# A hybrid encoder layer: the sums of w2's quarters, the second MLP product's order and the end of the kernel rearranged

## The chip, the cores and the metric

The kernel runs on one core of one Trainium2 chip. A core has a matrix engine (TensorE, PE, with its weight loads as PEld), a vector engine (VectorE, DVE), a scalar engine (ScalarE, ACT), a general engine (GpSimd, POOL) and a sync engine (SyncE, SP) that here issues transfers. The metric is the device time of one execution in microseconds (us), taken as the median of several runs.

## The reference, cut to what matters

One layer of a streaming encoder is applied to 1024 prompt tokens and to 8 x 16 sample tokens that carry states of earlier chunks; here all 1152 tokens go through together. All is float32.

```python
proj = x @ w_in                      # (1152, 1024) after a LayerNorm; its columns feed four mixers
mix  = concat(ssd(proj), mlstm(proj), rglru(proj), gla(proj))      # (1152, 2048); SSD and RG-LRU: causal conv4 first
x    = layer_norm(ALPHA * x + mix @ w_out, ln1_g, ln1_b)
hid  = square(relu(x @ w1 + b1))                                  # (1152, 4096)
x    = layer_norm(ALPHA * x + hid @ w2 + b2, ln2_g, ln2_b)        # written out, with 8 states per token kind
```

mLSTM, GLA and SSD are computed chunk by chunk (9 chunks of 128 tokens, the ninth is the sample), with a state carried from one prompt chunk to the next.

## The kernel before, in words

**How a product is made.** A float32 product is three products of reduced-precision parts: `mm3` issues hi·hi, hi·lo and lo·hi into one PSUM bank. The high part of an operand is a copy by ACT, the low part a subtraction by DVE (`wl<-wr,wh`, `mlo<-mr,mh`, `wo<-wq,wo`, `ol<-ar,oh`). So each weight passes SP (load), ACT (high part) and DVE (low part) before PE can use it.

**Stages**, with their place in the time of before:

- `dense_first` (to about 60 us): input LayerNorm, transposes, the first five column blocks of w_in in chunks of 384 tokens, three chunks (c = 0, 1, 2) each. Each block's `evac` empties its PSUM bank. For the first two blocks of the SSD convolution (`conv_block`), `evac` at c = 0 also transposes the carried conv states on PE (`pcs<-ident,cst`, line 737); they come by DMA into `cst`.
- SSD (to about 230), mLSTM (230 to 560), GLA (560 to 640), RG-LRU (640 to 860). PE works on the columns of w_in for a later mixer (`block`) while the small steps of the present mixer are put among them: `tick()` is called at fixed places of each block and hands out steps. In mLSTM a chunk i goes through `stA`, `stB` and `stC`; `stB` makes `y` (ACT, DVE, POOL), and `stC`, called three chunks behind `stA`, transposes `y` on PE (`py`). In GLA a chunk ends with the update of the state `St` on DVE and its scaled copies `glB`, which the next chunk's product reads.
- `w_out` and LN1 (865 to 1075): operands `mh`, `mlo` (of the mixed result `mr`) and `wh`, `wl`; `acc` gathers the products, and at the end each row tile of 128 tokens gets its LayerNorm (`st`, `rs`, ACT `acc<-acc,rs`), is stored to `xn_d` by SP and transposed on PE (`pt<-ident,acc`) for the MLP.
- The first MLP product, x @ w1 (1075 to 1440), by the seven-product scheme of Strassen and Winograd on quarters of each matrix, in 16 column blocks j. `mlp_a` and `mlp_b` issue a block's matmuls; `q_load` and `q_prep` load and prepare w1's quarters (`wq`, `wo`) two blocks ahead; `more()` is called among the matmuls and hands out a step of preparation. Results go through `hid` (DVE, ACT) to DRAM (`hid_d`) and sums of their quarters (`sq`) to `s_d`.
- The second MLP product, hid @ w2 (1440 to 1803), by the same scheme with products 1 to 7 of 8 units each (a unit is 256 of the inner dimension); the sums T1 to T4 of w2's quarters are read from DRAM (`t_d`). The sample tokens have a plain product, handed out with units of products 1, 0 (a name for units of the sample alone), 2 and 3.
- The end: LN2 of the last rows and their stores.

**The sums of w2's quarters** (`w2_sums`, lines 1631 to 1670): for each of 32 groups four loads of 128x256 by SP into buffers `w2q`, four subtractions on DVE, four stores to `t_d`, all 128 loads and 128 stores issued by SP. The steps are in the list `behind`, of which each `tick()` takes one; they lie from the start of mLSTM to the start of RG-LRU (225 to 668 us).

**What sets the order.** A scheduler of the tile framework orders each engine's instructions by a model of its own; only where `pinned` names an engine does that engine keep the order of the program. It names DVE, ACT and PE in `dense_first` (until line 360) and in one place of the MLP, and all four engines from line 2372 on, for the end. Between these, the order in which the code makes the instructions is only a wish. An engine works through its list in order: a waiting instruction holds up all behind it.

Of the kernel before, what the change touches and what calls it, by code (L numbers as in the profile page):

```python
# [39 lines left out]
STT = (7, 6)  # L40
NG5 = 0
PIN = 'VATG'
LOG = ((4, 0), (4, 1))
CHUNKS = (tuple(range(6)), (6, 7))
NQ = 3
HT = NTOK // 2
# [4 lines left out]
def tile_trunk(ctx: ExitStack, tc: tile.TileContext, I, O, dbg=None):  # L51
# [169 lines left out]
    behind = []  # L221
# [495 lines left out]
    def conv_block(store, key, st_in, nrow, ch0, wcol, bcol, act, o_p, o_s, early=False):  # L717
# [11 lines left out]
        def evac(c, ps):  # L729
            if c == 0:  # L730
                raw = S("raw", (P, SW))
                d["raw"] = raw
                V.memset(raw[:, 0:3], 0.0)
                sv = raw[:, 1027:1179].rearrange("p (b s) -> p b s", s=19)
                d["sv"] = sv
                cs = d["cs"] if early else load()
                pt = pm("pcs")
                T.transpose(pt[:, 0:24], cs[0:24, :], ident[0:24, 0:24])
                A.activation(sv[:, :, 0:3], pt[:, 0:24].rearrange("p (b j) -> p b j", j=3), AF.Copy)
            raw = d["raw"]  # L740
# [36 lines left out]
        def state():  # L777
            raw, sv = d["raw"], d["sv"]
            cs = Dt("cso", 27)
            A.activation(cs[:, 0:3], raw[:, PT:PT + 3], AF.Copy)  # L780
            A.activation(cs[:, 3:27].rearrange("p (b j) -> p b j", j=3), sv[:, :, LS:LS + 3], AF.Copy)
            pt = pm("pco")
# [298 lines left out]
    def ml_steps(h):  # L1081
# [22 lines left out]
        def stB(i):  # L1104
# [41 lines left out]
            y = Dt("y", P)  # L1146
            A.activation(y, ti[:, 0:P], AF.Square, scale=r[:, 0:1], accum_out=r[:, 1:2])
# [3 lines left out]
            G.tensor_scalar(y, ti[:, 0:P], r[:, 3:4], None, op0=OP.mult)  # L1151
            d["y", i] = y
# [36 lines left out]
        for s in range(NT + 3):  # L1189
            def f(s=s):  # L1190
# [6 lines left out]
                if 3 <= s <= NT + 2:  # L1197
                    stC(s - 3)
# [97 lines left out]
    def gl_steps(p):  # L1296
# [21 lines left out]
        def stB(i):  # L1318
# [3 lines left out]
            if i < 8:  # L1322
# [11 lines left out]
                if i:  # L1334
                    G.tensor_scalar(St, St, sc[:, 1, i:i + 1], None, op0=OP.mult)
                    V.scalar_tensor_tensor(St, pS, sc[:, 2, i:i + 1], St, op0=OP.mult, op1=OP.add)
                else:
                    V.tensor_scalar(St, pS, sc[:, 2, 0:1], None, op0=OP.mult)
                if i < 7:
                    for h in range(2):  # L1340
                        hs = slice(64 * h, 64 * h + 64)
                        V.tensor_scalar(glB[hs, h, :], St[hs], sc[hs, 0, i + 1:i + 2], None, op0=OP.mult)
# [129 lines left out]
    def rg_steps(j):  # L1472
# [15 lines left out]
        def gates(c):  # L1488
            def f():
# [7 lines left out]
                if c < 2:  # L1497
                    split(c + 1)
# [45 lines left out]
        return [g0] + [w] * 5 + [gates(0)] + [w] * 0 + [gates(1)] + [w] * 0 + [gates(2), e1, e2, e3]  # L1544
# [86 lines left out]
    def w2_sums():  # L1631

        out = []
        src = (("11", 0, 0), ("12", 0, 512), ("22", KF // 2, 512), ("21", KF // 2, 0))
        for k in range(KF // 2):
            for c in (0, 256):
                q = {}

                def load(k=k, c=c, q=q):
                    for nm, k0, c0 in src:  # L1640
                        q[nm] = C("w2q")[:, 0:256]
                        D.dma_start(q[nm], w2[(k0 + k) * P:(k0 + k + 1) * P, c0 + c:c0 + c + 256])

                def sub(dst, a, b, q=q):
                    V.tensor_tensor(q[dst], q[a], q[b], op=OP.subtract)

                def store(n, nm, k=k, c=c, q=q):
                    D.dma_start(t_d[n][k, :, c:c + 256], q[nm])

                def f2(sub=sub):  # L1650
                    sub("11", "12", "11")
                    sub("12", "22", "12")

                def f3(sub=sub, store=store):
                    store(0, "11")
                    store(2, "12")
                    sub("22", "22", "11")
                    sub("21", "22", "21")

                def f4(store=store):  # L1660
                    store(1, "22")
                    store(3, "21")

                if out:
                    last = out.pop()
                    out.append(lambda load=load, last=last: (last(), load()))
                else:
                    out.append(load)
                out += [lambda: None, f2, f3, f4]
        return out  # L1670

    behind.extend(w2_sums())
# [21 lines left out]
    while behind:  # L1694
        behind.pop(0)()
# [106 lines left out]
    def x_rest(k):  # L1802
# [11 lines left out]
        x_split("S4", k, a12)  # L1814

# [243 lines left out]

    for j in range(KF // 2):  # L2060
        def more():
            if prep[j] and j == 0:
# [8 lines left out]
        while j + 1 in prep and prep[j + 1]:  # L2071
            more()

# [56 lines left out]
    def lo_engine(p, u):  # L2130
        return G if (p, u - tail[0]) in LOG else V

    def w_prep(i):
        if i < len(units):
            p, u = units[i]
            opw[p, u] = parts(wr.pop((p, u)), lo_engine(p, u))

    def a_prep(i):
        if i < len(units):
            p, u = units[i]  # L2140
            if prods[p][0]:
                opa[p, u] = parts(ar.pop((p, u)), lo_engine(p, u))
# [18 lines left out]
    def sample(p, u):  # L2161
        if p in samp:
            h, g = samp[p]
            (ah, al), (wh, wl) = hs[u // 2], opw[p, u]
            for k in range(2):
                n = (u % 2) * 2 + k
                mm3(sps[h], (ah[:, g, n], al[:, g, n]), (wh[:, k], wl[:, k]),
                    u == k == g == 0, u == NU - 1 and k == 1 and g == 0)

    acc = {}  # L2170

    def part_of(p, t):

        nm, ix = {1: ("a1", None), 5: ("a5", None), 6: ("a6", None), 2: ("top", 0), 3: ("top", 1), 4: ("bot", 0),
                  7: ("bot", 1)}[p]
        key = (nm, t // 2 if ix is None else t)
        if key not in acc:
            acc[key] = S3(nm)
        return acc[key][:, t % 2 if ix is None else ix, :]

    def evac(p, t, ps, first):
        a = part_of(p, t)
        if first and p in (1, 5, 6):
            if t % 2:
                V.tensor_copy(a, ps)
            else:
                A.activation(a, ps, AF.Copy)
        else:
            V.tensor_tensor(a, a, ps, op=OP.subtract if p == 4 else OP.add)
# [10 lines left out]
    def res_make(i):  # L2200
# [3 lines left out]
        if 4 <= i < 8:  # L2204
            G.tensor_tensor(r[:, left], r[:, left], r[:, right], op=OP.subtract)
# [20 lines left out]
    def ln_b(i):  # L2226
        rs = lnrs[i]
        G.tensor_scalar(rs[:, 2:3], lnst[i][0][:, 24:25], rs[:, 1:2], -1.0, op0=OP.mult, op1=OP.mult)
        A.activation(row(i), row(i), AF.Identity, scale=rs[:, 1:2], bias=rs[:, 2:3])

    def ln_g(i):
        G.tensor_tensor(row(i), row(i), g2, op=OP.mult)

    def ln_stt(i, n):

        mean, rs = lnst[i][0][:, 24:25], lnrs[i]
        for cs in (left, right):
            a = row(i)[:, cs]
            if n == 0:
                V.scalar_tensor_tensor(a, a, mean, g2[:, cs], op0=OP.subtract, op1=OP.mult)  # L2240
# [212 lines left out]
```

## Time and profile before

| what | value |
|---|---|
| median of 3 runs | 1825.93 us (1824.7 to 1827.39) |
| profiled execution | 1824.16 us, span 1822.4 us |
| granted clock of PE, mean | 0.986 |
| PE busy | 1739.7 us (95%) |
| DVE busy | 1220.2 us (67%) |
| ACT busy | 748.3 us (41%) |
| POOL busy | 598.9 us (33%) |
| transfers | 252.5 MB, mean 139 GB/s |

Span is the time from the first to the last recorded event of the profiled execution; the device time of that same execution is 1.8 us longer. Busy shares are averages over stages that differ much: PE has no gap at all in some stages and stands often in others. Waits are inferred from semaphore events, with the releaser that came last.

### The profile page before, as it was taken

The numbers are of one execution on the slowest core, as the hardware profiler recorded it, in microseconds if no ns is written. First come the engines' busy times: TensorE is split into PE (matmuls) and PEld (weight loads), VectorE is DVE, ScalarE is ACT, GpSimd is POOL, SyncE is SP. The second block draws the span as 40 slices with busy tenths as digits, with TensorE's granted clock in tenths as the row PEclk, the third lists the DMA queues.
The fourth block names the chain that finished last, engine by engine and source line by source line (L and its number), as shares of the span: only waits on it lengthen the run. The fifth ranks groups of instructions, "written<-read, shape, count | busy, mean of one in ns | idle before, by whom it ended". The sixth has DMA issues, their size and how long they took to land. (4 is left out here: it accounts for less than half of the span.)

```text
span 1822.4 us, 28131 instructions
## 1 busy us (share of the span) xinstructions
PE 1739.7 (95%) x10439; PEld 1580.7 (87%) x10439; DVE 1220.2 (67%) x2263; ACT 748.3 (41%) x1463; POOL 598.9 (33%) x558
## 2 busy tenths in 40 slices
PE   6999999999999999998999998999999999999995
PEld 5898989999989889897887888999999988888884
DVE  6867776644573654678777579666666678856569
ACT  4544433332341322365542275444444443433331
POOL 1123223522531313234255026433333135430047
PEclk8999999999999999999999999999999999999998
DMA  5132343546434350211445222554443696664542
GB/s 167 49 108 62 106 126 91 182 150 182 150 109 142 108 146 12 78 39 61 160 131 187 76 93 82 186 180 167 145 145 128 220 324 212 214 235 164 186 150 93
DMA packets 226961, 252.53 MB, mean 139 GB/s; under 512 B 27834, under 2 KB 171340, under 8 KB 226824
## 3 DMA queue, kind: packets, MB, share of 16 engines
q1 hardware_dynamic: 213000, 215.08, 37.4%
q10 hardware_dynamic: 13824, 35.66, 5.1%
q8 instruction: 82, 1.34, 0.3%
q14 instruction: 55, 0.45, 0.1%
HBM read 172.59 MB, written 76.33 MB: 137 GB/s over the span
## 5 line engine op out<-in xcount | busy, mean ns | idle before, releaser
L66 PE MATMUL pd<-xh,wh 128*128 128x384 f32 x936 | 330.1, 353 | 2.6 <-ACT xh L66 2.3
L66 PE MATMUL pd<-xh,wl 128*128 128x384 f32 x936 | 318.7, 340 | 0.0
L66 PE MATMUL pd<-xl,wh 128*128 128x384 f32 x936 | 311.0, 339 | 0.3 <-DVE xl L66 0.3
L66 PE MATMUL pm<-xo,wo 128*128 128x288 f32 x1680 | 232.2, 297 | 9.3 <-DVE wo L66 6.1
L66 PEld LDWEIGHTS pm<-xo,wo 128*128 128x128 f32 x1680 | 227.1, 190 | 10.7 <-DVE wo L66 7.3
L66 PEld LDWEIGHTS pd<-xh,wh 128*128 128x128 f32 x936 | 177.8, 190 | 8.4 <-ACT xh L66 3.3
L66 PEld LDWEIGHTS pd<-xl,wh 128*128 128x128 f32 x936 | 177.2, 190 | 1.9 <-issue 1.0
L66 PEld LDWEIGHTS pd<-xh,wl 128*128 128x128 f32 x936 | 177.2, 189 | 0.1
L66 POOL TENSOR_TENSOR wq<-wq 128x512 f32<-128x512 f32 x64 | 94.5, 1477 | 168.6 <-DVE wo L66 152.6
L66 PE MATMUL pd<-xo,wo 128*128 128x288 f32 x1008 | 140.3, 296 | 0.1
L66 PEld LDWEIGHTS pd<-xo,wo 128*128 128x128 f32 x1008 | 136.8, 189 | 0.3 <-ACT hid L66 0.3
L66 DVE TENSOR_TENSOR wo<-wq,wo 128x512 fp32r<-128x512 f32 x112 | 102.0, 930 | 31.3 <-ACT wo L66 30.6
L66 DVE TENSOR_TENSOR ol<-w2r,oh 128x1024 fp32r<-128x1024 f32 x62 | 97.9, 1586 | 26.5 <-ACT oh L66 10.0
L66 DVE TENSOR_TENSOR wl<-wr,wh 128x1024 fp32r<-128x1024 f32 x63 | 87.6, 1392 | 26.3 <-ACT wh L66 17.9
L66 ACT ACTIVATE oh<-ar 128x1024 fp32r<-128x1024 f32 x56 | 59.2, 1057 | 105.1 <-DVE ol L66 29.1
L66 DVE TENSOR_TENSOR ol<-ar,oh 128x1024 fp32r<-128x1024 f32 x54 | 78.1, 1446 | 33.1 <-ACT oh L66 28.8
L66 ACT ACTIVATE oh<-w2r 128x1024 fp32r<-128x1024 f32 x64 | 67.2, 1052 | 58.6 <-DVE ol L66 31.4
L66 PE MATMUL pd<-oh,ol 128*128 128x512 f32 (+1 forms) x228 | 89.5, 392 | 0.0
L66 PE MATMUL pd<-ol,oh 128*128 128x512 f32 (+1 forms) x228 | 89.3, 392 | 0.0
L66 PE MATMUL pd<-oh 128*128 128x512 f32 (+1 forms) x228 | 89.0, 391 | 0.0
L66 PE MATMUL pm<-oh,ol 128*128 128x512 f32 (+1 forms) x224 | 87.8, 392 | 0.0
L66 PE MATMUL pm<-ol,oh 128*128 128x512 f32 (+1 forms) x224 | 87.6, 391 | 0.0
(420 smaller groups left out, 4019.6 us busy)
## 6 DMA issues: line engine op xcount, KB each, us to landing
wr<-in_w_in_dram SPq DMA_DIRECT2D x46, 512.0 KB
wq<-in_mlp_w_dram SPq DMA_DIRECT2D x72, 256.0 KB
hid_d<-hid ACTq DMA_DIRECT2D x32, 576.0 KB
w2q<-in_mlp_w_dram SPq DMA_DIRECT2D x128, 128.0 KB
t_d<-w2q SPq DMA_DIRECT2D x128, 128.0 KB
s_d<-sq ACTq DMA_DIRECT2D x64, 256.0 KB
w2r<-in_mlp_w_dram SPq DMA_DIRECT2D x32, 512.0 KB
w2r<-t_d SPq DMA_DIRECT2D x32, 512.0 KB
```

The lines of the kernel that those rows point to most:

```text
L66: r = f(*a, **k)
```

## The change

1. **The sums of w2's quarters** are made in the first MLP product: `w2_sums` gets three steps a group (load, subtract, store), four buffers of its own (`NWQ = 4`) in the MLP's pool, and its stores are issued by ACT. `more()` takes one step from j = 2 on; what is left comes after the last block. The `behind` list in `tick` is gone. T4 has the other sign, and product 4 is added where it was subtracted.
2. **The second MLP product**: before, all products ran over units 0 to 5, then over units 6 and 7, with their results emptied and gathered twice. Now products 1, 2, 6, 5, 3 run over all 8 units, one after the other (sample-only units `0` among those of 6), 4 and 7 over units 0 to 4. LN2 of rows 0 to 3 and of the sample is in a list `later`, of which each unit of the following products takes up to two steps.
3. **The end**: for each of the last four row tiles, product 7 and then product 4 over units 5 to 7, and then that row's LN2; the last row's product 4 in two halves of 256 columns.
4. **Smaller moves**: the conv states' transposes (`pcs`) at c = 2, not c = 0; the copies `cso` of the conv's new states a step before their transpose; mLSTM's `y` in place in `ti`, and `stC` four chunks behind `stA`, not three; in GLA the state's update at high priority; in RG-LRU the split of a chunk's operand for the gates a step earlier.

The diff, cut to its core:

```diff
-        if behind:
-            behind.pop(0)()
...
+            if c == 2:
                 pt = pm("pcs")
-                T.transpose(pt[:, 0:24], cs[0:24, :], ident[0:24, 0:24])
...
+                T.transpose(pt[:, 0:24], d["cs"][0:24, :], ident[0:24, 0:24])
...
-            st += [taps(c, 0, 2), taps(c, 2, 4)]
+            st += [taps(c, 0, 2), taps(c, 2, 4) if c < 2 else lambda c=c: (taps(c, 2, 4)(), kept())]
...
-            G.tensor_scalar(y, ti[:, 0:P], r[:, 3:4], None, op0=OP.mult)
-            d["y", i] = y
+            G.tensor_scalar(ti[:, 0:P], ti[:, 0:P], r[:, 3:4], None, op0=OP.mult)
+            d["y", i] = ti[:, 0:P]
...
-                if 3 <= s <= NT + 2:
-                    stC(s - 3)
+                if 4 <= s <= NT + 3:
+                    stC(s - 4)
...
+                with tc.high_priority():
+                    if i:
+                        V.scalar_tensor_tensor(St, pS, sc[:, 2, i:i + 1], St, op0=OP.mult, op1=OP.add)
...
-        return [g0] + [w] * 5 + [gates(0)] + [w] * 0 + [gates(1)] + [w] * 0 + [gates(2), e1, e2, e3]
+        return [g0] + [w] * 4 + [lambda: split(1), gates(0)] + [w] * 0 + [gates(1)] + [w] * 0 + [gates(2), e1, e2, e3]
...
+                def load(k=k, c=c, q=q):
+                    for nm, k0, c0 in src:
+                        q[nm] = s2.tile([P, 256], F32, tag="W", name="w2q", bufs=NWQ)
+                        D.dma_start(q[nm], w2[(k0 + k) * P:(k0 + k + 1) * P, c0 + c:c0 + c + 256])
+                def sub(dst, a, b, q=q):
+                    V.tensor_tensor(q[dst], q[a], q[b], op=OP.subtract)
+                def store(n, nm, k=k, c=c, q=q):
+                    A.dma_start(t_d[n][k, :, c:c + 256], q[nm])
+                def subs(sub=sub):
+                    sub("11", "12", "11")
+                    sub("12", "22", "12")
+                    sub("22", "22", "11")
+                    sub("21", "21", "22")
+                out += [load, subs, stores]
...
+    sums = w2_sums()
     for j in range(KF // 2):
         def more():
+            if j > 1 and sums:
+                sums.pop(0)()
...
-    order, order_end = (1, 5, 6, 4, 0, 7, 2, 3), (2, 3, 0, 1, 6, 5, 7, 4)
-    tail = CHUNKS[-1]
-    units = [(p, u) for us in CHUNKS for p in (order_end if us is tail else order) for u in us]
+    tail = (5, 6, 7)
+    units = ([(p, u) for p in (1, 2) for u in range(NU)] + [(p, u) for u in range(NU) for p in (6, 0)]
+             + [(p, u) for p in (5, 3) for u in range(NU)] + [(p, u) for p in (4, 7) for u in range(tail[0])]
+             + [(p, u) for p in (7, 4) for u in tail])
...
+    def second(t, parts_):
+        i = 4 + t
+        for cs in parts_:
+            ps = bank()
+            tile_prod(ps, 4, t, cs.start, cs.stop)
+            add(acc["bot", t][:, 0, cs], ps[:, cs])
             ln_stats2(i, cs)
         ln_a(i)
...
+    for t in range(4):
+        first(t)
+        if t:
+            ln_c(3 + t, left)
+            ln_c(3 + t, right)
+        second(t, lh if t == 3 else (left,))
+        if t < 3:
+            ln_b(4 + t)
+    ln_b(7, left)
+    ln_stt(7, right, 0)
+    ln_stt(7, right, 1)
+    ln_c(7, left)
```

How it moves instructions, at three places.

PE's order at the end of the first chunk of `dense_first`, before (`xh`, `xl` are the parts of the normed input, `wh`, `wl` those of w_in, `pd` a product's bank):

```order
L66 MATMUL pd<-xh_103,wh 128x384
L66 MATMUL pd<-xh_103,wl 128x384
L66 MATMUL pd<-xl_111,wh 128x384
L66 MATMUL pcs<-ident,cst 128x24
L66 MATMUL pd<-xl_111,wh 128x384
L66 MATMUL pcs<-ident,cst 128x24
L66 MATMUL pd<-xh_96,wh 128x384
L66 MATMUL pd<-xh_96,wl 128x384
```

And now, at the end of the third chunk:

```order
L63 MATMUL pd<-xh_103,wh 128x384
L63 MATMUL pd<-xh_103,wl 128x384
L63 MATMUL pd<-xl_111,wh 128x384
L63 MATMUL pcs<-ident,cst 128x24
L63 MATMUL pd<-xl_111,wh 128x384
L63 MATMUL pcs<-ident,cst 128x24
L63 MATMUL pd<-xl_111,wh 128x384
```

The two transposes have moved from the end of the first chunk to the end of the third, some 180 matmuls further on.

DVE's order in the last quarter of the `w_out` stage, before (`acc` gathers products, `mlo` is the low part of the mixed result):

```order
L66 TENSOR_TENSOR acc<-acc,pd 128x512
L66 TENSOR_TENSOR mlo<-mr,mh 128x1024
L66 TENSOR_TENSOR acc<-acc,pd 128x512 x2
L66 TENSOR_TENSOR mlo<-mr,mh 128x1024
L66 TENSOR_TENSOR acc<-acc,pm 128x512
L66 TENSOR_TENSOR acc<-acc,res 128x1024
L66 TENSOR_TENSOR acc<-acc,pm 128x512
L66 TENSOR_TENSOR mlo<-mr,mh 128x1024
```

And now, at the same place:

```order
L63 TENSOR_TENSOR mlo<-mr,mh 128x1024
L63 TENSOR_TENSOR w2q<-w2q 128x256 x3
L63 TENSOR_TENSOR acc<-acc,pd 128x512
L63 TENSOR_TENSOR w2q<-w2q 128x256
L63 TENSOR_TENSOR acc<-acc,pd 128x512
L63 TENSOR_TENSOR mlo<-mr,mh 128x1024
L63 TENSOR_TENSOR w2q<-w2q 128x256 x2
L63 TENSOR_TENSOR acc<-acc,pm 128x512
L63 TENSOR_TENSOR acc<-acc,res 128x1024
L63 TENSOR_TENSOR w2q<-w2q 128x256 x2
L63 TENSOR_TENSOR acc<-acc,pm 128x512
L63 TENSOR_TENSOR w2q<-w2q 128x256
```

The scheduler draws the first 10 or 11 of the 32 groups forward, out of the MLP's loop into the end of `w_out`, two loops ahead of where the code makes them; SP's loads of `w2q` stand there between those of `mr`, and ACT's stores to `t_d` between `mh` and `acc`. Some 9 more subtractions stand among the splits `xo` at the start of the MLP, the others among the first product's blocks.

DVE's order at the very end, before (`res` holds the rows, `st` and `rs` their statistics, `pd` and `pm` banks):

```order
L66 BN_STATS st<-res 128x6
L66 TENSOR_TENSOR res<-res,pm 128x256
L66 BN_STATS st<-res 128x6
L66 BN_AGGR st<-st 128x2
L66 TENSOR_SCALAR rs<-st 128x1
L66 SCALAR_TENSOR_TENSOR res<-res,st,g_17257 128x512 x2
L66 TENSOR_TENSOR res<-res,bb_17259 128x1024 x2
L66 SCALAR_TENSOR_TENSOR res<-res,rs,bb_17259 128x512 x2
L66 SCALAR_TENSOR_TENSOR res<-res,st,g_17257 128x512 x2
L66 SCALAR_TENSOR_TENSOR res<-res,rs,bb_17259 128x512 x2
```

And now:

```order
L63 BN_STATS st<-res 128x6
L63 TENSOR_TENSOR res<-res,pd 128x256
L63 BN_STATS st<-res 128x6
L63 BN_AGGR st<-st 128x2
L63 TENSOR_SCALAR rs<-st 128x1
L63 SCALAR_TENSOR_TENSOR res<-res,st,g_16539 128x512
L63 SCALAR_TENSOR_TENSOR res<-res,rs,bb_16541 128x512
L63 TENSOR_TENSOR res<-res,g_16539 128x512
L63 TENSOR_TENSOR res<-res,bb_16541 128x512
```

Behind the last addition of a product stood the last steps of four rows; now there are those of one row only.

## Rows read from the trace of the kernel before

**Rows 1.** the page, busy time of each engine

```profile
PE 1739.7 (95%) x10439; PEld 1580.7 (87%) x10439; DVE 1220.2 (67%) x2263; ACT 748.3 (41%) x1463; POOL 598.9 (33%) x558
```

**Rows 2.** PE in order: start, length, operation, [idle before <-releaser]

```profile
32.03 0.27 PE L66 MATMUL pcs<-ident,cst 24*128 24x24 f32 x1 [5.80 <-DMA cst<-in_state_ssd_conv_dram]
```

**Rows 3.** busy time by stretch: engines (count), PEclk, DMA share, GB/s

```profile
32.00:39.00 7.00, 6.97 (x24) 6.53 (x25) 0.00 (x0) 1.22 (x5) 0.00 (x0) 0.54 0.76 190
```

**Rows 4.** waits of PE, 60 to 230 us: total, times, longest

```profile
PE pco L66 <- ACT cso L66: 1.5, 1, 1.5
```

**Rows 5.** waits of PE, 230 to 640 us

```profile
PE py L66 <- POOL y L66: 7.3, 9, 2.4
PE pb L66 <- DVE E L66: 3.6, 6, 1.3
PE pb L66 <- DVE glB L66: 2.0, 3, 1.4
```

**Rows 6.** the tile w2q: ns min/median/max, first and last start; idle before it

```profile
L66 DVE TENSOR_TENSOR w2q<-w2q x128: 401/424/692, 230.9 to 665.7; 128x256 f32<-128x256 f32 x128
L1648 SPq DMA_DIRECT2D t_d<-w2q x128: 319/346/4178, 231.6 to 668.0; - x128
...
  DMA w2q<-in_mlp_w_dram: 32.4, 22
```

**Rows 7.** waits of PE, 800 to 1125 us

```profile
PE pgt L66 <- DVE gxl L66: 2.6, 3, 1.2
...
PE pt L66 <- ACT acc L66: 0.6, 1, 0.6
```

**Rows 8.** waits of DVE, 1001 to 1061 us

```profile
DVE mlo L66 <- ACT mh L66: 9.4, 3, 4.0
DVE acc L66 <- PE pd L66: 6.6, 5, 3.2
DVE acc L66 <- PE pm L66: 4.6, 3, 2.3
```

**Rows 9.** busy time by stretch, second half

```profile
1000.00:1075.00 75.00, 74.41 (x355) 61.25 (x354) 48.03 (x89) 29.80 (x41) 9.19 (x10) 1.00 0.22 81
1075.00:1125.00 50.00, 40.61 (x275) 39.09 (x274) 45.89 (x44) 32.15 (x57) 32.96 (x19) 0.90 0.18 53
1125.00:1440.00 315.00, 315.00 (x2377) 315.00 (x2376) 204.16 (x337) 152.94 (x269) 110.96 (x74) 1.00 0.48 164
1440.00:1803.00 363.00, 362.34 (x1594) 295.08 (x1592) 259.37 (x237) 138.23 (x142) 121.06 (x59) 1.00 0.58 198
```

**Rows 10.** the tile wq, whole run

```profile
L66 DVE TENSOR_TENSOR wo<-wq,wo x112: 635/688/1922, 1065.5 to 1416.6; 128x512 fp32r<-128x512 f32 x112
```

**Rows 11.** waits of DVE, 1130 to 1440 us

```profile
DVE sq L66 <- ACT hid L66: 36.3, 27, 2.3
DVE wo L66 <- ACT wo L66: 29.1, 27, 1.7
DVE hid L66 <- PE pm L66: 19.3, 25, 4.2
```

**Rows 12.** all engines in time order, the end

```profile
1802.27 0.28 PE L66 MATMUL pm<-ol,oh 128*128 128x256 f32 x1
...
1802.39 0.28 PE L66 MATMUL pm<-oh,ol 128*128 128x256 f32 x1
...
1808.14 0.40 DVE L66 TENSOR_TENSOR res<-res,pm 128x256 f32<-128x256 f32 x1
...
1809.46 3.56 DVE L66 SCALAR_TENSOR_TENSOR res<-res,st,g 128x512 f32<-128x512 f32 x2
...
1811.76 1.00 POOL L66 TENSOR_TENSOR rs<-rs,nhalf 128x1 f32<-128x1 f32 x1
...
1815.97 3.65 SPq L2243 DMA_DIRECT2D out_dram<-res  x4
...
1817.86 1.40 DVE L66 SCALAR_TENSOR_TENSOR res<-res,rs,bb 128x512 f32<-128x512 f32 x2
```

More of the change, by code (lines that the diff above doesn't have):

```diff
@@ L39 @@
 NS3 = 9
[L40 to L41 removed]
 PIN = 'VATG'
[L43 to L44 removed]
 NQ = 3
+NWQ = 4
 HT = NTOK // 2
@@ L1188, in ml_steps @@
         out = []
-        for s in range(NT + 3):
+        for s in range(NT + 4):
             def f(s=s):
@@ L1629, in pair @@
         nb[0] += 2
[L1631 to L1672, printed above, removed]
     ml_n0()
@@ L1814, in x_rest, with w2_sums, stores @@
         x_split("S4", k, a12)
+    def w2_sums():
+        out = []
+        src = (("11", 0, 0), ("12", 0, 512), ("22", KF // 2, 512), ("21", KF // 2, 0))
+        for k in range(KF // 2):
+            for c in (0, 256):
+                q = {}
+                def load(k=k, c=c, q=q):
[11 more added lines that the diff above has]
+                    sub("21", "21", "22")
+                def stores(store=store):
+                    for n, nm in enumerate(("11", "22", "12", "21")):
+                        store(n, nm)
+                out += [load, subs, stores]
+        return out
     wq, wo = {}, {}
@@ L2072, in tile_trunk @@
             more()
+    while sums:
+        sums.pop(0)()
     s2x.close()
@@ L2167, in sample @@
                 mm3(sps[h], (ah[:, g, n], al[:, g, n]), (wh[:, k], wl[:, k]),
-                    u == k == g == 0, u == NU - 1 and k == 1 and g == 0)
+                    u == k == g == 0, u == NU - 1 and k == g == 1)
     acc = {}
[L2172 to L2189, printed above, removed]
     def row(i):
@@ L2224, in ln_a @@
         rsqrt_to(rs[:, 1:2], rs[:, 0:1])
[L2226 to L2240, printed above, removed]
-            else:
-                V.scalar_tensor_tensor(a, a, rs[:, 1:2], bb2[:, cs], op0=OP.mult, op1=OP.add)
-                D.dma_start(out_of(i, cs), a)
@@ L2315, in tile_trunk @@
             V.tensor_tensor(ba, ba, b2, op=OP.add)
[L2316 to L2320 removed]
+        if i % 3 == 1:
+            if i > 1 and made:
+                res_make(made.pop(0))
+            if todo:
+                res_load(todo.pop(0))
+        if p == 5 and u == 0:
             g2 = vec_bc("g2", I["ln2_g"][0])
@@ L2323, in tile_trunk @@
         sample(p, u)
-        if end and p == 5:
-            break
+        for _ in range(2):
+            if later:
+                later.pop(0)()
         if not p:
             continue
-        if cu == 0:
+        if u == 0:
             banks = [bank() for _ in range(4)]
         (ah, al), (wh, wl) = opa[p, u], opw[p, u]
+        n = NU if p in (1, 2, 6, 5, 3) else NU - len(tail)
         for k in range(2):
@@ L2333, in tile_trunk, with tile_prod @@
                 ts = slice(t * P, (t + 1) * P)
[L2334 to L2336 removed]
+                mm3(banks[t], (ah[:, k, ts], al[:, k, ts]), (wh[:, k], wl[:, k]), u == k == 0, u == n - 1 and k == 1)
+        if u < n - 1:
             continue
[L2338 to L2362 removed]
+        for t in range(4):
+            evac(p, t, banks[t])
+        if p == 3:
+            for h, cs in enumerate((left, right)):
+                later.append(lambda h=h, cs=cs: (add(acc["smp"][:, h], sps[h]), ln_stats2(8, cs)))
+            later.append(lambda: ln_a(8))
+            later.append(lambda: ln_b(8))
+            later.append(lambda: ln_c(8))
+    while later:
+        later.pop(0)()
+    prep_to(len(units))
+    def tile_prod(ps, p, t, c0=0, c1=512):
         ts = slice(t * P, (t + 1) * P)
```

211 lines of the change are left out of this document (83 added, 128 removed).

## Prediction

> **What bounds the kernel now.** I read the page first. PE is busy for 1739.7 of 1822.4 us [rows 1], so in this trace at most 82.7 us can be won without taking matmuls away, and the change takes none away. What counts is therefore where PE stands, and for whom. Then I read PE's waits by stage, and busy time by stretch.
>
> Four places make up most of it. In the first stage PE stands 5.80 us for the DMA of `cst` [rows 2], and after it runs at a granted clock of 0.54 for 7 us [rows 3]. In mLSTM and GLA it waits in many small pieces, 7.3 us for `y`, 3.6 for `E`, 2.0 for `glB` [rows 5]. At the start of the MLP it is busy for 40.61 of 50 us, while DVE is busy for 45.89 [rows 9]. The end is bare: the last matmul begins at 1802.39 [rows 12], the span ends at 1822.4. In both MLP products PE has nearly no gap, 315.00 of 315 and 362.34 of 363 us [rows 9]; there nothing can be won and something lost. So the change takes work from stages with gaps and puts it into stages without any, and the question is whether the vector engine can hide it there.
>
> **The change part by part.** The sum is made against the profiled execution, 1824.16 us.
>
> *Conv states at c = 2.* The transposes stood in front of the second chunk's matmuls, and the data came at 32.03. They now come some 180 matmuls later, by when it has long landed. The 5.80 us go; what is late next (a weight's low part, by PE's order) these rows don't price, and I allow it 1 us. The stretch at 0.54 lost 7 x 0.46 = 3.2 us against full clock [rows 3], and a pause of 1 us instead of 5.8 before it may spare up to that. Ends: -4 to -9; I take -7.
>
> *`cso` earlier:* one wait of 1.5 us [rows 4]; 0 to -1.5, I take -1.
>
> *mLSTM and GLA.* DVE loses 128 subtractions of 0.424 us = 54 us here, and 32.4 us of standing for `w2q` in 22 waits [rows 6]; as DVE works in order, each of these held up the small chains behind it. `stC` one chunk later gives `y` a whole chunk more, the high priority brings `glB` forward. Against PE stand 7.3 + 3.6 + 2.0 = 12.9 us [rows 5]. Ends: 0 (the chains are late by themselves) and -13; the waits are short and many, as a shared in-order engine makes them, so I take -10. The 128 loads and 128 stores also leave SP here, which can only help the loads of w_in behind them.
>
> *RG-LRU's split a step earlier:* 2.6 us in three waits for `gxl` [rows 7]; 0 to -2.6, I take -2.
>
> *The end.* Before, behind the last matmul came the last addition at 1808.14, 5.7 us late because DVE had a backlog, and then 11 us of steps for four rows, to 1819.26; the span ends 3.1 us after that [rows 12]. Now from the addition to the first fused step it is the same 1809.46 - 1808.14 = 1.32 us. Two fused steps on half a row take 1.40 / 2 = 0.70 each [rows 12], while ACT does the other half, which waits for POOL's power (up to 1.00 us [rows 12]); then two more steps of the left half at 0.69, the price of a 128x512 subtraction [rows 10]. That is 1.3 + 1.4 + 1.4 = 4.1, and 3.1 to the end of the span, 7.2. DVE's backlog remains to be added. In the last row it has seven steps of 0.69 (three of product 7, four of the row before), then 0.40 and about 0.43 of the first half, 5.7 us; PE gives it 36 half-wide matmuls, which follow each other by 0.12 us [rows 12], 4.3 us. So DVE comes 1.4 us late, and with PE's last 0.3 and some small change the end takes about 9.7, not 1822.4 - 1802.7 = 19.7 us. Ends: -7 (POOL slows the two-input steps, and a 128x512 fused step takes 1.78 beside POOL, as the pair at 1809.46 [rows 12]) and -12; I take -10.
>
> *Sums of w2 in `w_out` and at the MLP's start.* By the order, 10 or 11 groups are made here, 42 subtractions of 0.424 = 18 us. DVE waits 9.4 + 6.6 + 4.6 = 20.6 us in this stretch [rows 8], so they fit in sum. But each group is a chain: SP's load, DVE, ACT's issue of the store, the store's end, and only then the next load, with four buffers where seven were shared. With seven a wait for a load cost 32.4 / 22 = 1.5 us [rows 6]. Behind a waiting subtraction stand `mlo` and `acc`, for which PE waits; behind a waiting load on SP stand the loads of `mr` and the stores of `xn_d`; behind a waiting store on ACT stand `mh` and the LayerNorm's `acc`, on which PE already waits 0.6 us [rows 7], so that there is no slack. At the MLP's start DVE has 4.1 us free of 50 [rows 9], and some 9 subtractions more (3.8 us) come. Ends: 0, and 11 groups at 1.5 us plus a few, +18. I take +6, a third.
>
> *Sums in the first MLP product.* Some 80 subtractions stay there. The stretch of 315 us holds about 15 blocks' worth of work, so a block is 21.0 us; DVE is busy for 204.16 / 15 = 13.6 of it [rows 9] and waits 7.4: 19.3 / 15 = 1.3 for PE, 65.4 / 15 = 4.4 for ACT (`sq`, `wo`) [rows 11], 1.7 for others. Added are 5.4 subtractions a block, 2.3 us at 0.424, 3.7 at the longest seen, 0.692 [rows 6]. If they fall into the waits, PE sees nothing: 0. If only the wait for PE gives room, a block gets 2.3 - 1.3 = 1.0 us longer, 15 us. ACT gets the issues of as many stores, 80 x 0.35 [rows 6] = 28 us of its 162 free [rows 9]. The transfers add 128 KB twice a subtraction, 20 MB to 52 (164 GB/s x 315 us), at a DMA share of 0.48 [rows 9]. Ends: 0 and +25; I take +5.
>
> Here a rule speaks against the change. A low-part subtraction of `wo` took 0.635 us at best and 1.922 at worst [rows 10], on the same shape, while POOL is busy for 110.96 of 315 us [rows 9]. The Trainium skill, page "SBUF — State Buffer", section "Who interferes with whom", says that a DVE instruction with two SBUF inputs contends with a GpSimd instruction that reads SBUF. The trace agrees: 1.922 / 0.635 is a factor of 3. The new subtractions are of that kind.
>
> In mLSTM and GLA none of them took over 0.692 us [rows 6]; at three times 0.401 one would take 1.2 us, a price that the slower rival carries and the forecast does not.
>
> *Second product.* PE gets the same matmuls in another order, the operands are prepared three units ahead as before, and the second emptying of the banks goes. DVE has 104 us free of 363 [rows 9], though between product 3's end and the end of the mains it must do the LayerNorm of five rows. Ends: 0 and +6; +1.
>
> Sum: -7 - 1 - 10 - 2 - 10 + 6 + 5 + 1 = -18, so 1824.2 - 18 = 1806. The median of the runs lies 1.8 us above the profiled execution, so the forecast is **1808 us**.
>
> **The rivals.**
>
> *The sums turn DVE into the bound of the first MLP product (slower).* At the contended price, a block's DVE work is 13.6 + 5.4 x 0.692 = 17.3 us, and if its waits for ACT and others (6.1) stay where they are, as waits in a chain do, the block takes 23.4 instead of 21.0 us: 2.4 x 15 = 36 us instead of 5. The sum is +13, 1839 us. At 1.2 us a subtraction a block would take 13.6 + 6.5 + 6.1 = 26.2 us, and the kernel near 1880. It decides from the point where added work and kept waits together exceed 7.4 us a block, and the kernel is slower from a loss of 23 us there. For it: PE at 315.00 of 315 with nothing to give, and POOL's 35%. Against it: DVE waits 19.3 us for PE here, so it is ahead, and the scheduler puts the subtractions where its model sees DVE wait.
>
> *The transfers' round trips hold up `w_out` (little gain).* All 11 groups cost 1.5 us and more, +18 instead of +6: -6, 1820. For it: four buffers, three engines in a ring, no slack at the LayerNorm. Against it: DVE's 20.6 us of waits there.
>
> *The mixers' waits stay (smaller gain).* If `y` and `E` are late through ACT and POOL and not through DVE, only the start and the end gain: -8, 1818. For it: the releaser of the largest is POOL. Against it: the 22 waits for `w2q` in the same stretch.
>
> *All that moves is hidden.* No loss in the MLP nor in `w_out`, and the bounds of the gains nearly reached: -18 - 12 - 5 = -35, 1790 us. For it: the added 54 us of DVE are a quarter of its idle time in these stages.
>
> **How the numbers follow.** Chances: the forecast (1798 to 1816) 0.45; all hidden 0.13; the mixers' waits stay 0.10; round trips 0.15, half of it within the bound of no change; DVE the bound 0.17. A difference of under 0.2%, 3.7 us, is not told from none. So faster 0.45 + 0.13 + 0.10 + 0.07 = 0.75, same 0.08, slower 0.17. The range from 1790 to 1834 leaves out a little of the best case, and most of the slower one.
>
> **What would show it.** Right: no wait of PE for `cst` and a granted clock near 1 from 32 to 39 us; `py<-y` and `pb<-E` below 4 us together; the span ending 9 to 11 us after the last matmul; PE nearly without gaps from 1125 us on as counted before. Wrong: waits of PE for `wo` in the MLP's blocks, with `w2q` subtractions of 0.7 us and more on DVE; waits of DVE for `w2q`, of SP for a free buffer, or of PE for `mlo`, `wl` or `acc` in `w_out`, worth more than 20 us together; or a wait of PE for `ol` or for a bank in products 4 and 7, where DVE does the LayerNorm.

## The result and the profile after

The changed kernel took 1874.83 us (median of 4 runs, 1871.92 to 1877.81), the kernel before 1825.88 in the same session: a ratio of 1.027, 95% interval 1.0253 to 1.0287. It is 49 us slower where 18 us less were forecast, beyond the range of 1790 to 1834. The profiled execution took 1874.46 us, with a span of 1872.7.

The page of the changed kernel, busy time of each engine, to be read against [rows 1]:

```profile
PE 1761.6 (94%) x10445; PEld 1593.5 (85%) x10445; DVE 1197.0 (64%) x2269; ACT 749.8 (40%) x1459; POOL 524.9 (28%) x528
```

The span grew by 50.3 us: PE stands 28.4 us longer, and its busy time grew by 21.9, with six matmuls more in the trace and a mean granted clock of 0.981 instead of 0.986. To see where, I took from the tile view, in which each group of instructions has the start of its first and last, five marks that both kernels have. Three of them, each in the kernel before and then in the changed kernel (the group, ns min/median/max, first and last start):

```profile
L66 PE MATMUL pd<-wh,mh x172: 387/393/500, 851.5 to 1070.5; 128*128 128x512 f32 x172
```

```profile
L63 PE MATMUL pd<-wh,mh x172: 387/392/774, 837.3 to 1071.7; 128*128 128x512 f32 x172
```

```profile
L66 ACTq DMA_DIRECT2D hid_d<-hid x32: 326/326/407, 1133.2 to 1448.5; - x32
```

```profile
L63 ACTq DMA_DIRECT2D hid_d<-hid x32: 326/327/516, 1139.9 to 1495.2; - x32
```

```profile
L66 PE MATMUL pd<-oh x228: 280/393/404, 1447.3 to 1800.7; 128*128 128x512 f32 x112, 128*128 128x256 f32 x2
```

```profile
L63 PE MATMUL pd<-oh x236: 274/393/404, 1492.6 to 1862.4; 128*128 128x512 f32 x112, 128*128 128x256 f32 x6
```

| up to | before | after | after minus before | of which in this stretch | forecast |
|---|---|---|---|---|---|
| first SSD state product (`pS<-xdw`) | 145.8 | 135.7 | -10.1 | -10.1 | -8 |
| first matmul of w_out | 851.5 | 837.3 | -14.2 | -4.1 | -12 |
| first store of `hid_d` (w_out, LN1, MLP's start) | 1133.2 | 1139.9 | +6.7 | +20.9 | +6 |
| first matmul `pd<-oh` of product two | 1447.3 | 1492.6 | +45.3 | +38.6 | +5 |
| last matmul | 1802.4 | 1862.6 | +60.2 | +14.9 | +1 |
| end of the span | 1822.4 | 1872.7 | +50.3 | -9.9 | -10 |

The start and the end of the kernel came close to the forecast. The stretch that had stood at half the clock [rows 3], and the one ahead of it, now (busy time by stretch; PE, PEld, DVE, ACT, POOL, then granted clock, DMA share, GB/s):

```profile
26.00:32.00 6.00, 5.34 (x32) 4.75 (x31) 4.75 (x20) 1.80 (x5) 2.50 (x6) 1.00 0.21 49
32.00:39.00 7.00, 6.97 (x45) 6.59 (x44) 5.12 (x11) 4.52 (x10) 0.00 (x0) 1.00 0.77 194
```

PE stands 0.57 us where it stood 5.80 [rows 2], and the clock stays at 1.00. The end, in order of time, to be read against [rows 12]:

```profile
1862.61 0.28 PE L63 MATMUL pd<-oh,ol 128*128 128x256 f32 x1
...
1864.12 0.40 DVE L63 TENSOR_TENSOR res<-res,pd 128x256 f32<-128x256 f32 x1
...
1865.43 0.74 DVE L63 SCALAR_TENSOR_TENSOR res<-res,st,g 128x512 f32<-128x512 f32 x1
...
1866.62 0.75 DVE L63 SCALAR_TENSOR_TENSOR res<-res,rs,bb 128x512 f32<-128x512 f32 x1 [0.44 <-POOL rs L63]
...
1868.38 0.69 DVE L63 TENSOR_TENSOR res<-res,g 128x512 f32<-128x512 f32 x1 [1.01 <-ACT res L63]
1869.10 0.69 DVE L63 TENSOR_TENSOR res<-res,bb 128x512 f32<-128x512 f32 x1
1869.82 0.33 SPq L2207 DMA_DIRECT2D out_dram<-res  x1
```

DVE's last addition begins 1.5 us after the last matmul (1.4 was worked out), and the span ends 10.1 us after that matmul, not 20.0. From the addition to the end of DVE's last step it is 5.7 us, not the 4.1 worked out: DVE stands 0.44 us for POOL's power and 1.01 us for ACT's half.

The middle is another matter. The tile `w2q` now, to be read against [rows 6]:

```profile
L63 DVE TENSOR_TENSOR w2q<-w2q x128: 372/425/1651, 993.1 to 1434.6; 128x256 f32<-128x256 f32 x128
...
  DMA w2q<-in_mlp_w_dram: 52.7, 31
  issue: 14.9, 7
```

The subtractions are as short as before (median 0.425 us, mean 0.444), but DVE stands 52.7 + 14.9 us in front of them (`issue` is standing for which the profile shows no releaser). In `w_out`, ACT in order of time (ACTq is a transfer that ACT issues):

```profile
1005.10 1.06 ACT L63 ACTIVATE mh<-mr 128x1024 fp32r<-128x1024 f32 x1 [6.40 <-DMA mr<-mix_d]
1005.16 18.49 ACTq L63 DMA_DIRECT2D t_d<-w2q  x11
1023.96 1.24 ACT L63 ACTIVATE acc<-acc,rs 128x1024 f32<-128x1024 f32 x1 [17.80 <-DMA t_d<-w2q]
```

Eleven stores stand there in ACT's list between two steps, each waiting for its subtraction; ACT does nothing else for 17.8 us, and the LayerNorm's step behind them is late. PE's wait for it grew from 0.6 us [rows 7] to 9.5, of which 6.4 in one piece. In the first MLP product, waits of DVE from 1130 to 1440 us (total, times, longest), to be read against [rows 11]:

```profile
DVE w2q L63 <- DMA w2q<-in_mlp_w_dram: 38.2, 18, 4.7
DVE wo L63 <- ACT wo L63: 30.1, 30, 1.7
DVE w2q L63 <- issue: 14.9, 7, 3.2
```

DVE's wait for PE, 19.3 us in before, is gone from the list: DVE was ahead of PE and is now behind it. PE's own waits from 1125 to 1460 us show for whom it stands:

```profile
PE pm L63 <- DVE hid L63: 15.0, 9, 3.4
PE pd L63 <- DVE hid L63: 6.4, 6, 2.8
PE pm L63 <- DVE wo L63: 3.2, 2, 2.2
```

Between the two marks of this stretch PE stands 23.9 us in all, where it never stood before. The other 14.7 of the 38.6 us are a longer busy time; the granted clock there is 0.98 on average, before 1.00, which by an estimate (352.7 x 0.02) makes up half of them.

The loss in product two lies in its first 50 us; behind 1540 us PE waits for nothing there. POOL, DVE and PE at that place:

```profile
1516.26 8.51 POOL L63 TENSOR_TENSOR res<-res,ga 128x1024 f32<-128x1024 f32 x3 [30.98 <-DMA b<-in_mlp_b_dram]
1524.74 9.93 POOL L63 TENSOR_TENSOR res<-res,ba 128x1024 f32<-128x1024 f32 x3
```

```profile
1515.34 0.69 DVE L63 TENSOR_SCALAR ga<-ga 128x1024 f32<-128x1024 f32 x1 [7.66 <-DMA ga<-in_ln_g_dram]
1516.62 2.59 DVE L63 TENSOR_SCALAR ba<-ba 128x1024 f32<-128x1024 f32 x1 [0.58 <-DMA ba<-in_ln_b_dram]
1519.25 3.30 DVE L63 TENSOR_TENSOR ba<-ba,b 128x1024 f32<-128x1024 f32 x1
1522.47 3.38 DVE L63 TENSOR_TENSOR ol<-ar,oh 128x1024 fp32r<-128x1024 f32 x1
```

```profile
1529.19 0.79 PE L63 MATMUL pd<-ol,oh 128*128 128x512 f32 x1 [6.14 <-DVE ol L63]
```

The loads of `ga`, `ba` and `b2` had moved from unit 4 to unit 0, those of the first rows from unit 4 to unit 1, and POOL's steps on these rows from unit 6 to unit 4. DVE waits 7.7 us for `ga`, then POOL's six steps on `res` run beside it, and a subtraction with a median of 1.22 us takes 3.38:

```profile
L63 DVE TENSOR_TENSOR ol<-ar,oh x56: 1211/1224/3433, 1486.1 to 1820.6; 128x1024 fp32r<-128x1024 f32 x56
```

PE stands 6.1 us for `ol`, and from 1520 to 1540 its granted clock is 0.74.

### The profile page after: what moved, and what is told of

The parts are those of the page before. It is cut to its first block, busy times and chain, and to the rows that moved or that the text cites. A ratio compares the mean times of both kernels' runs of the same rounds, so it can differ in the third digit from the quotient of the medians.

```text
span 1872.7 us, 28069 instructions
## 1 busy us (share of the span) xinstructions
PE 1761.6 (94%) x10445; PEld 1593.5 (85%) x10445; DVE 1197.0 (64%) x2269; ACT 749.8 (40%) x1459; POOL 524.9 (28%) x528
## 5 line engine op out<-in xcount | busy, mean ns | idle before, releaser
L63 PE MATMUL pm<-xo,wo 128*128 128x288 f32 x1680 | 240.8, 302 | 31.1 <-DVE hid L63 15.4
L63 PEld LDWEIGHTS pm<-xo,wo 128*128 128x128 f32 x1680 | 231.9, 193 | 37.2 <-DVE hid L63 18.9
L63 PE MATMUL pd<-xo,wo 128*128 128x288 f32 x1008 | 145.8, 301 | 7.1 <-DVE hid L63 6.4
L63 DVE TENSOR_TENSOR wo<-wq,wo 128x512 fp32r<-128x512 f32 x112 | 108.8, 985 | 36.5 <-ACT wo L63 36.4
L63 ACT ACTIVATE wo<-wq 128x512 fp32r<-128x512 f32 x112 | 66.8, 624 | 116.6 <-POOL wq L63 51.8
L63 DVE TENSOR_TENSOR ol<-w2r,oh 128x1024 fp32r<-128x1024 f32 x64 | 91.7, 1436 | 33.4 <-ACT oh L63 19.6
L63 DVE TENSOR_TENSOR ol<-ar,oh 128x1024 fp32r<-128x1024 f32 x56 | 84.3, 1505 | 42.9 <-ACT oh L63 37.5
L63 DVE TENSOR_TENSOR w2q<-w2q 128x256 f32<-128x256 f32 x128 | 56.8, 444 | 71.1 <-DMA w2q<-in_mlp_w_dram 52.7
L63 POOL TENSOR_TENSOR rs<-rs,nhalf 128x1 f32<-128x1 f32 x27 | 18.2, 674 | 285.7 <-DVE rs L63 285.6
```

Source lines behind the costliest of these rows:

```text
L63: r = f(*a, **k)
```

## The experiments

Three theories. **R**: the sums' ring (load by SP, subtraction on DVE, store by ACT, and the next load only behind the store's end) makes in-order engines wait. **C**: the added subtractions themselves, stretched by POOL, make DVE the bound. **O**: product two loses by its own new order. Each kernel's loss is read from three stretches: w_out's first matmul to the first `hid_d` store; from there to product two; and the whole, beside the kernel before on the same chip.

| kernel | median us, ratio (95% interval) | w_out to hid_d | to product two |
|---|---|---|---|
| before | 1825.88 | 281.7 | 314.1 |
| changed | 1874.83, 1.027 (1.0253 to 1.0287) | 302.6 | 352.7 |
| e1_sums_alone | 1881.31, 1.0304 (1.0284 to 1.0325) | 299.7 | 353.1 |
| e2_rest | 1820.73, 0.9974 (0.9964 to 0.9984) | 282.4 | 314.1 |
| e3_stores_sp | 1865.88, 1.022 (1.0203 to 1.0238) | 298.6 | 351.6 |
| e4_gate | 1873.82, 1.0276 (1.025 to 1.0303) | 284.0 | 367.5 |
| e5_start | 1810.4, 0.9924 (0.9905 to 0.9942) | 282.9 | 314.2 |
| e6_no_stores | 1861.13, 1.0196 (1.0176 to 1.0217) | 298.8 | 338.2 |
| e7_no_subs | 1843.36, 1.0101 (1.0083 to 1.0118) | 300.2 | 319.8 |
| e8_subs | 1838.91, 1.0078 (1.0056 to 1.01) | 301.5 | 313.9 |
| e9_mixers_old | 1809.37, 0.9926 (0.9913 to 0.994) | 281.6 | 314.2 |
| e10_subs_in_mlp | 1843.33, 1.0113 (1.0099 to 1.0127) | 282.3 | 335.8 |
| e11_deep | 1887.77, 1.0353 (1.0338 to 1.0368) | 299.5 | 369.9 |
| e12_eight | 1869.98, 1.0264 (1.0238 to 1.029) | 282.0 | 368.9 |
| e13_five_wq | 1819.62, 0.9974 (0.9963 to 0.9985) | 283.1 | 314.4 |

**The sums alone, and the rest alone.** On the kernel before, only the sums' move; on the changed kernel, only the sums back in their old place:

```diff
+            if j > 1 and sums:
+                sums.pop(0)()
```

```diff
+        if behind:
+            behind.pop(0)()
```

> The kernel before with the first part of the change alone: the sums of w2's quarters in the first MLP product, four buffers, stores by ACT; the old order of the second product, the old end, the old small parts. Theory R (the ring): a group's load, subtraction, store and the wait for the store's end go round four buffers, and DVE, ACT and SP stand in it in order, so w_out loses about 14 us and the MLP's start and first product about 44; 1826 + 58 = about 1884. Under R the loss in the first 80 us of the second product (15 us in the changed kernel) stays out if it comes from the new order of that product (theory O); if it comes from loads that the sums hold back on SP, it is here too, and the time is about 1899. Theory C (contention with POOL makes the subtractions long): the same time, but the w2q subtractions on DVE then have a mean of 0.8 us or more, and DVE does not wait for w2q loads.

> The changed kernel with its sums put back where they were in the kernel before (beside mLSTM and GLA, seven shared buffers, all transfers by SP): all other parts of the change. If the second product's new order costs 15 us by itself (theory O), the start gives 10, the mixers about 0 to 4 (less than the 4 seen, since the sums are back), the end 10: about 1819. If those 15 us came from the sums (theory R), about 1804.

1881 and 1821. The sums alone cost 55 us and the rest alone gains 3 to 7 (ratio 0.9964 to 0.9984), so the whole loss is theirs, but for product two: in e2 it still takes 367.1 us from first to last matmul, against 355.1 before and 358.6 in e1. That part is theory O. Theory C's sign, a mean of 0.8 us a subtraction, is not there (0.457 in e1). In the mixers, the sums' leaving alone gave 7.4 us up to w_out's first matmul, though 87 us of DVE's time (work and waits) went with them.

**Where the ring holds up work.** Stores by SP instead of ACT; and the sums held out of w_out:

```diff
-                    A.dma_start(t_d[n][k, :, c:c + 256], q[nm])
+                    D.dma_start(t_d[n][k, :, c:c + 256], q[nm])
```

> The changed kernel with the stores of the sums issued by SP, not by ACT. Theory R with ACT as the place where the ring holds up work (ACT stood 17.8 us behind stores before a LayerNorm step in w_out, and 50 us in the MLP): about 15 to 40 us faster than the changed kernel, 1835 to 1860. Theory R with DVE's wait for the loads as the place (52.7 us in 31 waits): no faster, 1875 or more, since SP now issues a load only behind the stores of the group before.

```diff
+    for _ in range(NWQ):
+        wt = s2.tile([P, 256], F32, tag="W", name="w2q", bufs=NWQ)
+        V.tensor_copy(wt[:, 0:1], X[7][:, 0:1])
     sums = w2_sums()
```

> The changed kernel with one thing more: the four w2q buffers are first written by a small copy from the MLP's operand x, so that no group can be drawn forward into w_out. Theory R: w_out gets its 14 us back, but 11 groups more fall into the first MLP product, which lost 39 us with 21 groups, 1.9 us a group: 1875 - 14 + 20 = about 1881. If the loss in the MLP comes from something else than the groups made there (a late start from w_out), about 1861 or less.

With ACT free of the stores, 9 us came back, 4 of them up to `hid_d` and 1 in the first product, far from the 15 to 40 of the one theory. With the sums held back, w_out was as fast as before and the first product lost 53 us for 32 groups instead of 39 for about 20, 1.7 and 1.9 us a group. So the loss in the MLP does not come from w_out's late end; a group costs where it is made. But PE does not stand for the same thing in the two. Its waits in e4, from 1060 to 1490 us:

```profile
PE pm L63 <- ACT hid L63: 22.5, 8, 6.5
PE pd L63 <- ACT oh L63: 15.5, 1, 15.5
...
PE pd L63 <- ACT hid L63: 6.7, 3, 5.1
...
PE pm L63 <- DVE hid L63: 0.2, 1, 0.2
```

In the changed kernel PE stands for DVE's `hid`, in e4 for ACT's, and 15.5 of e4's 53 us are one wait at the head of product two, while the last groups are still made; without it a group costs 1.2 us. So ACT, with the stores in its list, can be the place of the harm as well. The 50 us in the MLP that the expectation of e3 puts down to ACT's stores stand in the trace behind `s_d<-sq`, the stores of another part of the MLP, behind which ACT stood 39.5 us in the kernel before too.

**What in a group costs.** On e2_rest, a second and idle set of sums beside the MLP, with one of its three parts left out. No stores; no subtractions; subtractions alone, four for each of 32 loads:

```diff
-                out += [load, subs, stores]
+                out += [load, subs]
```

> e2_rest (sums in their old place) with a second, idle set of loads and subtractions in the first MLP product where the change puts its own: 128 loads by SP, 128 subtractions in place, four buffers, no store. Leaves the store out of the ring. If the store's end (theory R: a load waits for the store before it) is what makes DVE wait, the waits for loads shrink and most of the 58 us stays out: about 1835. If the loads alone are too slow for an in-order DVE: 1860 or more. Theory C (DVE's added work): about 1875, as in the full change.

```diff
+                out += [load, stores]
```

> e2_rest with a second set of loads and stores there, and no subtraction: 128 loads by SP, 128 stores by ACT into spare memory, four buffers. DVE does nothing for it. Theory R with DVE as the place where the ring does its harm: about 1830. With ACT, which stands in front of each store until the load has landed: 1850 or more. Theory C: 1821.

```diff
+                    for n in range(4):
+                        V.tensor_tensor(xw, q["11"], xc, op=OP.subtract)
```

> e2_rest with 128 idle subtractions of 128x256 there, four for each of 32 loads into three buffers, no store: DVE has the added work of the change and next to no wait. Theory R: DVE hides it, 1821 to 1830. Theory C: 1860 or more.

In the first MLP product, loads and subtractions cost 24.1 us, loads and stores 5.7, subtractions nothing; all three cost 38.6. But the scheduler did not leave the same amount there: in the changed kernel 79 of the 128 subtractions lie in that product (20 groups), in e6 56 (14 groups), in e7 64 loads with their stores (16 groups). By group that is 1.9 us for all three, 1.7 for loads and subtractions, 0.4 for loads and stores. So a group costs nearly as much without its stores, and e6, at 1861 us, came out as its second case, loads that are too slow for an in-order DVE: the store's end, as theory R has it, is not needed for the loss. Transfers that DVE has nothing to do with are cheap there. As a whole, e7 (1843 us) and e8 (1839) came out at none of their expected values, since 17.8 and 19.1 us fell in w_out and at the MLP's start, which they had not counted. For e6, the tile `xq` (as `w2q`):

```profile
L63 DVE TENSOR_TENSOR xq<-xq x128: 367/424/1629, 1003.3 to 1256.3; 128x256 f32<-128x256 f32 x128
...
  DMA xq<-in_mlp_w_dram: 38.2, 22
```

Of the 38.2 us that DVE stands for loads here, 27.4 lie in the first product. In e8 the scheduler had drawn nearly all subtractions ahead, between 1000 and 1162 us, where they cost 19.1 us without any wait; 13 of the 128 lie in the first product, so it says nothing of the MLP. e10 holds them back into it, by the same copy as in e4_gate:

```diff
+        wt = s2.tile([P, 256], F32, tag="W", name="xq", bufs=NWQ)
+        V.tensor_copy(wt[:, 0:1], X[7][:, 0:1])
```

> e8_subs with the first use of its buffers held back until the MLP's operand x is made, so that all 128 idle subtractions lie in the first MLP product and its start (in e8 they lay from 1000 to 1162 us, and cost 10 us in w_out and 9 at the MLP's start, nothing later). Still one load per four subtractions, no store. Theory R (only waiting subtractions hurt in the MLP): the stretch from the first hid_d store to the second product takes 314 to 319 us, the whole 1821 to 1835. Theory C (DVE's added work by itself): 330 us or more there, 1840 or more.

They cost 21.7 us there, against R. The tile `xw` of e10, and 50 us of the stretch in which they lie, with 50 us behind it:

```profile
L63 DVE TENSOR_TENSOR xw<-xq,xc x128: 408/425/1658, 1116.9 to 1270.5; 128x256 f32<-128x256 f32 x128
...
  DMA xq<-in_mlp_w_dram: 0.9, 2
```

```profile
1200.00:1250.00 50.00, 43.30 (x306) 41.99 (x305) 48.94 (x94) 19.35 (x34) 12.48 (x9) 0.97 0.48 161
...
1300.00:1350.00 50.00, 50.00 (x379) 50.00 (x378) 34.82 (x57) 23.98 (x43) 18.72 (x13) 1.00 0.45 152
```

Without waits the scheduler packs 128 subtractions into 154 us, 17.5 a block; DVE is busy for 48.9 of 50 us and PE for 43.3, and once they are done PE is at 50 of 50 again. So theory C holds at that density: 0.7 us for four subtractions. In the changed kernel, with about 5.3 a block, DVE is busy for 30 to 38 of 50 us, and C alone is not what is seen there; what bare subtractions cost at that density, no run shows. Work alone (0.7) and transfers alone (0.4) do not add up to the 1.7 us of a group in e6. The rest is put down here to DVE's standing for loads; this is an estimate by difference, from runs in which the work lies at different densities.

**Is it the ring's depth?** Groups of 128 columns with eight buffers; then eight full buffers, with two fewer for w1's quarters, and the control for that:

```diff
-            for c in (0, 256):
+            for c in range(0, 512, 128):
```

> The changed kernel with its sums in groups of 128 columns and eight buffers, the same 4 KB a partition: two groups in flight where there was one, with twice as many loads, subtractions, stores, each half as large. Theory R: DVE waits less for loads; the first MLP product loses 15 to 25 us instead of 39, the whole about 1860. If the number of transfers is what costs (each taking an engine's issue and a fixed time): 1880 or more.

```diff
-NR = 7
+NR = 5
-NWQ = 4
+NWQ = 8
```

> e4_gate (all sums held back into the MLP) with eight buffers of 256 columns, two whole groups in flight, room made by five buffers for w1's quarters instead of seven. e4_gate took 367.5 us from the first hid_d store to the second product, with four. If the ring's depth is what makes DVE wait: 335 to 350 us there, and the whole 1840 to 1858. If depth does not matter (e11_deep, where it came with twice as many transfers, gained nothing): 365 us or more, 1872 or more.

> The control of e12_eight: e2_rest (sums in their old place) with five buffers for w1's quarters instead of seven. If they are enough: 1821, the stretch from hid_d to the second product 314 us. What it loses is to be taken off e12_eight.

Neither helped. e11 lost 65 us against the kernel before where the change lost 49, e12 took 368.9 us where e4_gate took 367.5, and the control lost nothing. DVE's waits in e12 from 1105 to 1490 us:

```profile
DVE w2q L63 <- DMA w2q<-in_mlp_w_dram: 49.2, 29, 3.8
```

With twice the buffers DVE stands 49.2 us in front of the loads, where e4_gate has 32.9 (and 16.7 put down to the stores). My theory that the depth is what counts falls. What stays open is why the loads land so late: SP waits 149.5 us for the stores' end in e12 too (189.8 in e4_gate), and the stores stand in ACT's list behind other waiting work; but in e6, without stores, DVE waits for its loads too. A list in which the subtractions stand a fixed distance behind their loads was not tried.

**Product two, and the mixers' small parts.** e2 with `ga`, `ba`, `b2` and the rows' loads as late as in before; then also the old `y` and `stC`:

```diff
-        if i == 0:
+        if i == 4:
             ga = vec_bc("ga", I["ln1_g"][0], ALPHA)
...
+        if i >= 4 and i % 3 == 1 and todo:
+            res_load(todo.pop(0))
+        if i >= 5 and i % 3 == 0 and len(made) > len(todo):
+            res_make(made.pop(0))
```

> e2_rest with the start of the second product as in the kernel before: the loads of ga, ba and b2 at unit 4 instead of 0, the rows' loads and their steps on POOL from unit 4 and 6 on instead of 1 and 4. Theory O1 (what cost 15 us in the new second product is this work put at its start, where POOL's three steps of res slow DVE's subtractions so that PE waits 7.9 us for ol and then runs at a lower clock): the second product takes about 356 us instead of 370, 1821 - 13 = about 1808. Theory O2 (the order of the products by itself, two products with the sample's share one after the other, whose transfers fill the queues): no change, 1820.

```diff
-                if 4 <= s <= NT + 3:
-                    stC(s - 4)
+                if 3 <= s <= NT + 2:
+                    stC(s - 3)
```

> e5_start with mLSTM's y in a buffer of its own again and stC three chunks behind stA, as in the kernel before. From the first matmul of w_out, e2_rest gained 8.4 us on the kernel before, 10.1 of them at the start: so the small parts in the mixers lost 1.7 us, and in the changed kernel 3.3 (4.1 gained behind the start, 7.4 with the sums' move alone). If the later stC is what loses: 1807. If it is the GLA's high priority or RG-LRU's split: 1810, no change.

1810: product two takes 356.4 us again, so O1 has the place right, with 10.7 of the 12 us that e2 lost there; O2, the order of the products by itself, has no more than the rest. The edit puts back the loads and POOL's steps together; what DVE's wait for `ga` costs and what POOL beside DVE costs is not told apart. PE's waits in e5's product two:

```profile
PE ps L63 <- DVE ol L63: 1.1, 1, 1.1
PE pd L63 <- DVE res L63: 0.4, 1, 0.4
```

e9 is 1809.4, not told from e5; `stC` a chunk later neither gains nor loses. Both beat the kernel before by 0.6 to 0.95%: the change without the sums' move, and with product two's first loads left late.

## Why the prediction was wrong, by its own steps

- *Conv states at c = 2, and `cso`*: -7 and -1 forecast, -10.1 measured up to SSD's first state product. The gap of 5.80, the 3.2 us of half clock behind it and the 1.5 us for `cso` went nearly whole; I had taken 8 of these 10.5.
- *Mixers*: -10 and -2 forecast, -4.1 measured. By e1 the sums' leaving gave 7.4. PE's wait for `y`, 7.3 us in [rows 5], is 1.3 now, but `E` stays at 3.1, and new ones came: 2.0 for `c`, 1.8 for `wv`, 1.5 for `Ce`. In e9 with the old `y` it is 7.4 again, and the time is the same: a wait that goes is not time won when the next one follows. RG-LRU's split brought nothing: PE's wait for `gxl` is 2.8 us in three waits, 2.6 before. The rival that the mixers' waits stay was nearer.
- *The end*: -10 forecast, -9.9 measured. DVE's lateness came as worked out (1.5 us for 1.4). The steps behind it took 1.6 us more than worked out, through two waits that the sum had not priced; some 0.8 us of unnamed change in the sum covered half of that, which is luck.
- *Sums in w_out and at the MLP's start*: +6 forecast with an end at +18; +20.9 measured. I saw the ring, the three engines behind it and the missing slack, and then took a third of the upper end. By e8, 116 bare subtractions in and just behind w_out cost 19.1 us; by e7, half of the loads and stores alone 17.8. Either part alone costs most of it, so this loss is not the ring's alone.
- *Sums in the first MLP product*: +5 forecast with an end at +25, +38.6 measured. This is the step that failed. I compared added work (2.3 us a block) with DVE's waits (7.4), as if the work could fall into them, and priced waits for loads only in w_out, at 1.5 us each. In the first MLP product I put them at nothing, without a reason. There DVE stood 38.2 + 14.9 = 53.1 us in front of the subtractions, 3.5 us a block; with the work that is 5.8, and the waits for ACT on `wo` stayed (30.1 against 29.1). What gave way were the waits for PE (1.3 a block) and for `sq` (36.3 us before, 3.0 now, 2.2 a block): 21.0 + 5.8 - 1.3 - 2.2 = 23.3 us a block, where 352.7 / 15 = 23.5 were measured. These are the changed kernel's own waits, so this is an account and not a forecast. That the sums' move costs this is shown by e1 and e2, that a group costs 1.7 us without its stores by e6; how much of it is waiting and how much work is only estimated, and why the loads land so late stays open.
- *The slower rival* had the place and a block of 23.4 us, but by long subtractions; they were short (mean 0.444 us). That its block agrees with the 23.5 measured is luck. It had 0.17 of the chance.
- *Product two*: +1 forecast, +14.9 measured. I spoke of prepared operands and of DVE behind product 3, and not of the lines of the diff that move the loads from unit 4 to units 0 and 1 and POOL's steps from unit 6 to unit 4. This is where the rule that I weighed does hold: the Trainium skill, "SBUF — State Buffer", "Who interferes with whom", says that a DVE instruction with two SBUF inputs contends with a GpSimd instruction that reads SBUF; the trace agrees: the same subtraction takes 1.22 us alone and 3.38 beside POOL.

## What to carry to other kernels

Work that waits for a transfer is not priced by its busy time when it is put on an in-order engine that feeds the bound: count each wait, and ask what stands behind it. A stage in which that engine shows idle time may have less to give than it shows: some waits are kept when other work is put beside them (here those for `wo`, while those for `sq` gave way). And in a diff with one large move, price the small lines too: a few loads and steps taken earlier cost 11 us here, and putting them back raised the gain of the rest of the change from 5 to 13 us.

## What was not expected of the hardware

A DVE subtraction of 128x1024 with both inputs in SBUF takes 1.22 us, and at the start of product two 3.36 to 3.39 while POOL runs two-input steps of the same size on SBUF; even `ba`'s scale with one input took 2.59 us there, where `ga`'s, just ahead of POOL's steps, took 0.69. In e7, 64 loads and 64 stores more in the first MLP product (17 MB) cost it 5.7 us in 314, at a DMA share of 0.63.
